# Feature-major product: a block's high-part matmuls first, then its low-part matmuls

## The chip, the cores and the metric

The kernel runs on one core of a Trainium2 chip. The metric is the device time in microseconds from launch to end, median of three runs. Every input and output is fp32.

## What is computed

A two-layer model on 256 tokens of width 2048. Layer 0 mixes an HGRN2 recurrence with latent attention, layer 1 is a retention layer; each is followed by a convolution FFN of width 5632 and by a gated per-layer embedding:

```
h = x
for i in range(2):
    u = rmsnorm(h, norm_mix[i])
    h = h + (even_mixer(u, ...) if i == 0 else odd_mixer(u, ...))
    h = h + conv_ffn(rmsnorm(h, norm_ffn[i]), w_gate[i], w_up[i], conv_w[i], conv_b[i], w_down[i])
    gate = sigmoid(rmsnorm(h, norm_ple[i]) @ ple_w_gate[i])
    h = h + (p[i] @ ple_w_proj[i]) * gate
```

What matters here are the large matrix products in it: the projections of both mixers, three products in each FFN and two in each embedding. Some 520 MB of fp32 weights are read from HBM, each value once.

## The kernel before, in words

Activations are kept with the features on the partitions and the 256 tokens (`T`) along the free dimension, in pieces of 128 features. A product in near-fp32 precision is made of matmuls in the type fp32r: each operand is split into a high part (the value rounded to fp32r) and a low part (the rest), and three of the four partial products are summed: high with high, high with low, low with high. An activation piece `x` holds its high part in columns 0 to 255 and its low part in columns 256 to 511.

`load_w` (L136 to L143) brings a block of weights: SP's queue loads `raw` (four buffers), ACT makes the high part `wh` by a cast (L140, three buffers), and DVE makes the low part `wl` by a subtraction (L142, three buffers). `blocks_of` (L145 to L151) yields these blocks for one group of output features, four pieces of the inner dimension to a block (`KB` = 4).

`gemm_fm` (L153 to L166) computes 256 output features, 128 in each of two PSUM banks. For each of the four pieces `kc` of a block and each bank `j` it issues two matmuls, each with a weight load of its own: the high part of the weights with all 512 columns of `x` (L163, here called *hi*), which gives high times high in the bank's first half and high times low in its second, and right behind it the low part of the weights with the 256 high columns of `x` (L164, *lo*), summed into the first half. A block is so eight pairs, hi and lo in turn. In the product of the per-layer input (`px`) the inner dimension has two pieces, and a block is four pairs.

`gemm_fm` serves the output projections of both mixers, the query, key and gate projections of layer 1, all of the FFN's products and the embedding's. Two other products stand beside it: `gemm_fm1` (L168 to L184), in which one bank takes both halves and all matmuls have 256 columns (L178, L180, L181), and `gemm_tm` (L186 to L202), in which the activations are the loaded operand and all matmuls have 512 columns (L197, L198, L199).

After each block `pump()` lets chains of small steps go on (norm statistics, rotary parts, the recurrence, attention), so that their small matmuls (such as L871, L894 and L895 in layer 1) come in between large ones. After a product, `evac` (L204 to L209) adds the halves of a bank by a copy on ACT (L208) and an add on DVE (L209), or `residual` (L310 to L315) adds both halves to `h`. PSUM has five buffers for large products (`mm`) and three for small ones. The order on ACT and DVE is set when the kernel is built and isn't quite the order of the text: the cast of a block stands ahead of the copies of the product before it where there is room.

Of the kernel before, what the change touches and what calls it, by code (L numbers as in the profile page):

```python
# [15 lines left out]
PSUM = bass.MemoryType.PSUM  # L16

P = 128
T = 256
# [10 lines left out]
CH = 64  # L30
# [16 lines left out]

# columns of the packed vectors
_VEC = (
# [12 lines left out]

# columns of the packed constant matrices
_MAT = (
# [12 lines left out]
def hybrid_kernel(ctx, tc, io):  # L77
    nc = tc.nc
# [31 lines left out]

# [1 line left out]
    active = []  # L112
# [21 lines left out]

# [1 line left out]
    def load_w(src, width):  # L136
# [8 lines left out]
    def blocks_of(blocks, n, width, kb, sub=None):  # L145
        """The loaded parts of one group's weights, kb chunks of K in a block, sub of them to a load."""
        sub = sub or kb
        for k0 in range(0, n, sub):
            k1 = min(n, k0 + sub)
            o = (k0 % kb) * width  # L150
            yield range(k0, k1), load_w(blocks[k0 // kb][:, o:o + (k1 - k0) * width], (k1 - k0) * width)  # L151

    def gemm_fm(blocks, xs):  # L153
        """[features, tokens] of 256 features, a bank for each 128: products with the weights' hi (and lo with
        the activations' hi) in columns 0..T, with the activations' lo in columns T..2T."""
        ps = [psum.tile([P, 2 * T], F32, tag="mm", name="mm", bufs=5) for _ in range(2)]
        n = len(xs)
        for ks, (wh, wl) in blocks_of(blocks, n, 2 * P, KB):
            for kc in ks:
                x = xs[kc]  # L160
                for j in range(2):
                    o = ((kc - ks[0]) * 2 + j) * P
                    nc.tensor.matmul(ps[j], wh[:, o:o + P], x, start=(kc == 0), stop=False)  # L163
                    nc.tensor.matmul(ps[j][:, 0:T], wl[:, o:o + P], x[:, 0:T], start=False, stop=(kc == n - 1))  # L164
            pump()
        return ps  # L166

    def gemm_fm1(blocks, xs, ncol=2, kb=KB, sub=None):  # L168
        """[features, tokens] of ncol * 128 features in one bank."""
        ps = psum.tile([P, ncol, T], F32, tag="mm", name="mm", bufs=5)  # L170
        n = len(xs)
        for ks, (wh, wl) in blocks_of(blocks, n, ncol * P, kb, sub):
            for kc in ks:
                x = xs[kc]
                for j in range(ncol):
                    o = ((kc - ks[0]) * ncol + j) * P
                    w = wh[:, o:o + P]
                    nc.tensor.matmul(ps[:, j], w, x[:, 0:T], start=(kc == 0 and j == 0), stop=False,  # L178
                                     skip_group_check=True)
                    nc.tensor.matmul(ps[:, j], w, x[:, T:2 * T], start=False, stop=False, skip_group_check=True)  # L180
                    nc.tensor.matmul(ps[:, j], wl[:, o:o + P], x[:, 0:T], start=False,  # L181
                                     stop=(kc == n - 1 and j == ncol - 1), skip_group_check=True)
            pump()
        return ps  # L184

    def gemm_tm(blocks, xs, sub=None):  # L186
        """[tokens, 512 features], a bank for each half of the tokens."""
        ps = [psum.tile([P, 512], F32, tag="mm", name="mm", bufs=5) for _ in range(2)]
        n = len(xs)
        for ks, (wh, wl) in blocks_of(blocks, n, 512, 2, sub):  # L190
            for kc in ks:
                x = xs[kc]
                o = (kc - ks[0]) * 512
                for m in range(2):
                    xh = x[:, m * P:(m + 1) * P]
                    xl = x[:, T + m * P:T + (m + 1) * P]
                    nc.tensor.matmul(ps[m], xh, wh[:, o:o + 512], start=(kc == 0), stop=False)  # L197
                    nc.tensor.matmul(ps[m], xh, wl[:, o:o + 512], start=False, stop=False)  # L198
                    nc.tensor.matmul(ps[m], xl, wh[:, o:o + 512], start=False, stop=(kc == n - 1))  # L199
            if ks[-1] % 4 == 3:  # L200
                pump()
        return ps  # L202

    def evac(ps, dst):  # L204
        """dst = the two halves of each bank added."""
        tmp = npool.tile([P, 2, T], F32, tag="evt", name="evt", bufs=2)
        for j in range(2):
            nc.scalar.copy(tmp[:, j], ps[j][:, T:2 * T])  # L208
            nc.vector.tensor_tensor(dst[:, j], ps[j][:, 0:T], tmp[:, j], op=ALU.add)  # L209
# [7 lines left out]
    def split(dst, src, gain=None):  # L217
        """dst = [hi | lo] of src * gain."""
        if gain is None:
            nc.scalar.copy(dst[:, 0:T], src)  # L220
            nc.vector.tensor_tensor(dst[:, T:2 * T], src, dst[:, 0:T].bitcast(F32), op=ALU.subtract)
        else:
            nc.scalar.activation(dst[:, 0:T], src, AF.Copy, scale=gain)
            nc.vector.scalar_tensor_tensor(  # L224
                dst[:, T:2 * T], src, gain, dst[:, 0:T].bitcast(F32), op0=ALU.mult, op1=ALU.subtract)
# [4 lines left out]
    def rstd_from(ps_col, shape, n, factor=1.0):  # L230
        """(sum of squares / n + eps) ** -0.5 * factor of a small PSUM tile."""
        w = shape[1]
# [8 lines left out]
    def diagonals(r, order):  # L241
        """[hi | lo] of the columns of r, each on a diagonal."""
        n = len(order)
# [11 lines left out]
    def bcast_rows(dg, dst):  # L255
        """dst[:, i * 128 + t] = dg[t, 0, i, t] + dg[t, 1, i, t] on every partition."""
        n = dg.shape[2]
        ps = small([P, 512], "sm_bc")
        for half in range(2):
            nc.tensor.matmul(ps[:, 0:n * P], ones_r, dg[:, half].rearrange("p a b -> p (a b)"),  # L260
                             start=(half == 0), stop=(half == 1))
        nc.scalar.copy(dst, ps[:, 0:n * P])

    def token_stats(acc, n, wait=0):
        """1 / rms of each token from squares [features, any, tokens]: as columns and on every partition."""
        r = {}
# [19 lines left out]
    def norm_squares(i, state):  # L286
        """Squares of one finished pair of chunks of the residual stream."""
        acc = state[0]
# [25 lines left out]

# [1 line left out]
    def sin_of(dst, ang, phase, tpool):  # L316
# [29 lines left out]

# [1 line left out]
    def ffn_and_ple(i, st):  # L348
        rs = token_stats(st[0], D, 2)
        xs = st[1]  # L350
        cw, cb = f"cw{i}", f"cb{i}"
        st = new_norm()
        with tc.tile_pool(name=f"ffn{i}", bufs=2, reuse_waits="tile") as fp:
# [69 lines left out]
            def embed_last(pps):  # L423
                """The last group of all, a chunk at a time, on as short a path as can be."""
                n = NC // 2 - 1
# [24 lines left out]

# [1 line left out]
    def lower_bounds(pool):  # L452
        """Softmax over the two rows of logits: [lower bound, 1 - lower bound]."""
        lbt = pool.tile([P, 4, HG_HEADS], F32, name="lbt", bufs=1)
# [15 lines left out]
    def hgrn_pair(pool, hp, f, q, gt, lbc, hvs, mix):  # L470
        """The recurrence of two heads, in chunks of CH tokens."""
        def t2(tag, bufs=1):
# [53 lines left out]
        yield  # L526
        # states after chunks 0 and 2 from rows 0..63, after chunk 1 from rows 64..127, in banks of their own
        pse = small([P, 2, 2, P], "sm_se")
# [49 lines left out]
    def even_mixer(rs, xs):  # L578
        st = new_norm()
        mix_a, mix_b = {}, {}  # L580
        with tc.tile_pool(name="low", bufs=2) as low:
            kpe = low.tile([P, 1, T], F32, name="kpe", bufs=1)
            with tc.tile_pool(name="l0a", bufs=2) as pool:
# [34 lines left out]

                # low-rank projections and their norms
                def low_rank(ps, n, gain, acc, chunks):  # L620
# [34 lines left out]
    def mla(pool, kpe, ckv, cq, rkv, rqa, mix):  # L655
        """Starts the chains of all heads."""
        cos, sin = rope_t["mla"]
# [11 lines left out]
        def pair_rstd(sq, factor):  # L669
            """1 / rms of each (token, head of a pair) from the squares of both heads."""  # L670
            ps = small([P, 512], "sm_hs")
# [6 lines left out]

        # the keys' rotary part, the same for all heads
        key = {}  # L680
# [129 lines left out]

# [1 line left out]
    def odd_mixer(st):  # L812
# [123 lines left out]

# [1 line left out]
    class Arriving:  # L938
        """Chunks of the normed input, loaded and split on their first use."""
        def __init__(self):  # L940
# [27 lines left out]

# [1 line left out]
def _blocks(w, ncols, kb):  # L970
    """[K, N] -> [N / ncols, K / (kb * 128), 128, kb * ncols]: one contiguous piece for each load."""
    K, N = w.shape
# [4 lines left out]
def _cols(v):  # L977
    """[n * 128] -> [128, n]"""
    return np.asarray(v).reshape(-1, P).T
# [103 lines left out]
```

## Time and profile before

| | us |
|---|---|
| median of three runs | 2906.72 |
| lowest and highest run | 2904.05, 2907.08 |
| the profiled execution, first to last instruction (its span) | 2900.2 |
| TensorE matmul busy | 2888.3 |
| TensorE weight load busy | 2525.0 |
| VectorE (DVE) busy | 1957.8 |
| ScalarE (ACT) busy | 1397.4 |
| GpSimd (POOL) busy | 88.6 |

The times of the runs take in what lies around the span, so the profiled execution is known by its span: 2900.2 us, 6.5 us below the median of the runs. Matmuls are pipelined, so their records overlap, and a matmul's price in a stretch is the distance from its start to the next one's. A line such as L163 has a row for the matmul (PE) and one for its weight load (PEld).

### The profile page before, as it was taken

The numbers are of one execution on the slowest core, as the hardware profiler recorded it, in microseconds if no ns is written. First come the engines' busy times: TensorE is split into PE (matmuls) and PEld (weight loads), VectorE is DVE, ScalarE is ACT, GpSimd is POOL, SyncE is SP. The second block draws the span as 40 slices with busy tenths as digits, with TensorE's granted clock in tenths as the row PEclk, the third lists the DMA queues.
The fourth block names the chain that finished last, engine by engine and source line by source line (L and its number), as shares of the span: only waits on it lengthen the run. The fifth ranks groups of instructions, "written<-read, shape, count | busy, mean of one in ns | idle before, by whom it ended". The sixth has DMA issues, their size and how long they took to land.

```text
span 2900.2 us, 42896 instructions
## 1 busy us (share of the span) xinstructions
PE 2888.3 (100%) x16865; PEld 2525.0 (87%) x16865; DVE 1957.8 (68%) x2857; ACT 1397.4 (48%) x1848; POOL 88.6 (3%) x123
## 2 busy tenths in 40 slices
PE   9999999999999999999999999999999999999999
PEld 7999888888888888888888888888888888888888
DVE  8676777676557766786666556666777655777666
ACT  6554554444334444565444344444444433444444
POOL 2111400000000000000000000000000000000000
PEclk9999999999999999999999999999999999999999
DMA  6444355555555555555555555555555555555554
GB/s 220 170 159 160 103 180 180 191 187 189 185 182 191 185 187 189 177 199 177 177 177 180 188 180 179 174 176 188 191 184 182 191 186 188 187 183 190 186 185 167
DMA packets 148812, 525.72 MB, mean 181 GB/s; under 512 B 16640, under 2 KB 18432, under 8 KB 148608
## 3 DMA queue, kind: packets, MB, share of 16 engines
q1 hardware_dynamic: 148608, 522.96, 53.5%
q8 instruction: 132, 2.16, 0.3%
q14 instruction: 72, 0.59, 0.1%
HBM read 520.80 MB, written 2.10 MB: 180 GB/s over the span
## 4 chain that ended last, share of the span: by engine, by line
PE 88%; ACT 0%; DVE 0%; issue 0%
PE mm L163 53%; PE mm L164 27%; PE mm L198 2%; PE mm L197 2%; PE mm L199 2%; PE sm_ro L894 1%; PE sm_ra L871 0%; PE sm_ro L895 0%; PE sm_col L274 0%; PE sm_sc L767 0%; PE sm_bc L260 0%; PE mm L181 0%; PE mm L180 0%; PE mm L178 0%; PE sm_sc L766 0%; PE sm_ao L795 0%
## 5 line engine op out<-in xcount | busy, mean ns | idle before, releaser
L142 DVE TENSOR_TENSOR wl<-raw,wh 128x1024 fp32r<-128x1024 f32 (+1 forms) x1000 | 1206.0, 1210 | 722.9 <-ACT wh L140 721.1
L140 ACT CAST wh<-raw 128x1024 fp32r<-128x1024 f32 (+1 forms) x1000 | 1036.7, 1037 | 1210.7 <-PE mm L163 815.7
L163 PE MATMUL mm<-xs,wh 128*128 128x512 f32 x4320 | 1527.8, 398 | 0.0
L164 PE MATMUL mm<-xs,wl 128*128 128x256 f32 x4320 | 1212.4, 281 | 0.0
L163 PEld LDWEIGHTS mm<-xs,wh 128*128 128x128 f32 x4320 | 811.6, 188 | 199.6
L164 PEld LDWEIGHTS mm<-xs,wl 128*128 128x128 f32 x4320 | 815.7, 189 | 0.3
L163 PE MATMUL mm<-hs,wh 128*128 128x512 f32 x1408 | 497.6, 397 | 0.0
L164 PE MATMUL mm<-hs,wl 128*128 128x256 f32 x1408 | 395.6, 281 | 0.0
L163 PEld LDWEIGHTS mm<-hs,wh 128*128 128x128 f32 x1408 | 264.7, 188 | 65.4
L164 PEld LDWEIGHTS mm<-hs,wl 128*128 128x128 f32 x1408 | 264.3, 188 | 0.0
L208 ACT COPY evt<-mm 128x256 f32<-128x256 f32 x302 | 111.3, 374 | 205.7 <-PE mm L164 205.7
L163 PE MATMUL mm<-xo,wh 128*128 128x512 f32 x512 | 179.9, 393 | 0.0
L178 PE MATMUL mm<-xs,wh 128*128 128x256 f32 x560 | 160.0, 286 | 0.5 <-ACT wh L140 0.5
L181 PE MATMUL mm<-xs,wl 128*128 128x256 f32 x560 | 158.6, 283 | 0.5 <-DVE wl L142 0.4
L180 PE MATMUL mm<-xs,wh 128*128 128x256 f32 x560 | 158.4, 283 | 0.0
L164 PE MATMUL mm<-xo,wl 128*128 128x256 f32 x512 | 144.9, 283 | 0.0
L198 PE MATMUL mm<-wl,xs 128*128 128x512 f32 x320 | 125.7, 393 | 2.7 <-DVE wl L142 2.6
L199 PE MATMUL mm<-wh,xs 128*128 128x512 f32 x320 | 124.8, 391 | 0.6 <-DVE xs L224 0.6
L197 PE MATMUL mm<-wh,xs 128*128 128x512 f32 x320 | 124.5, 391 | 0.0
L163 PEld LDWEIGHTS mm<-xo,wh 128*128 128x128 f32 x512 | 96.2, 188 | 22.1
L178 PEld LDWEIGHTS mm<-xs,wh 128*128 128x128 f32 x560 | 107.3, 192 | 1.6 <-ACT wh L140 0.9
L181 PEld LDWEIGHTS mm<-xs,wl 128*128 128x128 f32 x560 | 107.3, 192 | 0.8 <-DVE wl L142 0.8
(264 smaller groups left out, 2369.9 us busy)
## 6 DMA issues: line engine op xcount, KB each, us to landing
raw<-in_wg SPq DMA_DIRECT2D x176, 512.0 KB, 3.3
raw<-in_wu SPq DMA_DIRECT2D x176, 512.0 KB, 4.1
raw<-in_wd SPq DMA_DIRECT2D x176, 512.0 KB, 4.0
raw<-in_w_oqk SPq DMA_DIRECT2D x64, 512.0 KB, 3.3
raw<-in_w_ov SPq DMA_DIRECT2D x64, 512.0 KB, 3.3
raw<-in_w_og SPq DMA_DIRECT2D x64, 512.0 KB, 3.2
raw<-in_w_oo SPq DMA_DIRECT2D x64, 512.0 KB, 3.2
raw<-in_wpg SPq DMA_DIRECT2D x60, 512.0 KB, 3.9
```

The lines of the kernel that those rows point to most:

```text
L140: nc.scalar.copy(wh, raw)
L142: nc.vector.tensor_tensor(wl, raw, wh.bitcast(F32), op=ALU.subtract)
L163: nc.tensor.matmul(ps[j], wh[:, o:o + P], x, start=(kc == 0), stop=False)
L164: nc.tensor.matmul(ps[j][:, 0:T], wl[:, o:o + P], x[:, 0:T], start=False, stop=(kc == n - 1))
L178: nc.tensor.matmul(ps[:, j], w, x[:, 0:T], start=(kc == 0 and j == 0), stop=False, skip_group_check=True)
L180: nc.tensor.matmul(ps[:, j], w, x[:, T:2 * T], start=False, stop=False, skip_group_check=True)
L181: nc.tensor.matmul(ps[:, j], wl[:, o:o + P], x[:, 0:T], start=False, stop=(kc == n - 1 and j == ncol - 1), skip_group_check=True)
L197: nc.tensor.matmul(ps[m], xh, wh[:, o:o + 512], start=(kc == 0), stop=False)
L198: nc.tensor.matmul(ps[m], xh, wl[:, o:o + 512], start=False, stop=False)
L199: nc.tensor.matmul(ps[m], xl, wh[:, o:o + 512], start=False, stop=(kc == n - 1))
L208: nc.scalar.copy(tmp[:, j], ps[j][:, T:2 * T])
L894: nc.tensor.matmul(pso[:, j], v[:, b, 0, d], at[:, c, 0:T], start=(n == 0), stop=False)
```

## The change

Within a loaded block, the loop over the pieces and banks is run twice: first with all hi matmuls, then with all lo matmuls. The operands, the banks, the columns and the flags of each matmul stay as they were: `start` on the first piece's hi, `stop` on the last piece's lo. The order of the sums in a bank changes with the order of the matmuls. Comments and docstrings were dropped as well, which changes no instruction.

```diff
     def gemm_fm(blocks, xs):
...
         for ks, (wh, wl) in blocks_of(blocks, n, 2 * P, KB):
             for kc in ks:
-                x = xs[kc]
                 for j in range(2):
                     o = ((kc - ks[0]) * 2 + j) * P
-                    nc.tensor.matmul(ps[j], wh[:, o:o + P], x, start=(kc == 0), stop=False)
-                    nc.tensor.matmul(ps[j][:, 0:T], wl[:, o:o + P], x[:, 0:T], start=False, stop=(kc == n - 1))
+                    nc.tensor.matmul(ps[j], wh[:, o:o + P], xs[kc], start=(kc == 0), stop=False)
+            for kc in ks:
+                for j in range(2):
+                    o = ((kc - ks[0]) * 2 + j) * P
+                    nc.tensor.matmul(ps[j][:, 0:T], wl[:, o:o + P], xs[kc][:, 0:T], start=False, stop=(kc == n - 1))
             pump()
         return ps
```

## Rows read from the trace of the kernel before

**Rows 1.** The page: the span, TensorE's busy time, the granted clock by slices.
```profile
span 2900.2 us, 42896 instructions
...
PE 2888.3 (100%) x16865; PEld 2525.0 (87%) x16865; DVE 1957.8 (68%) x2857; ACT 1397.4 (48%) x1848; POOL 88.6 (3%) x123
...
PEclk9999999999999999999999999999999999999999
```

**Rows 2.** The page: the chain that ended last, by engine and line.
```profile
PE 88%; ACT 0%; DVE 0%; issue 0%
PE mm L163 53%; PE mm L164 27%; PE mm L198 2%; PE mm L197 2%; PE mm L199 2%; PE sm_ro L894 1%; PE sm_ra L871 0%; PE sm_ro L895 0%; PE sm_col L274 0%; PE sm_sc L767 0%; PE sm_bc L260 0%; PE mm L181 0%; PE mm L180 0%; PE mm L178 0%; PE sm_sc L766 0%; PE sm_ao L795 0%
```

**Rows 3.** Groups by line: form, count | busy us, mean ns | idle before.
```profile
L163 PE MATMUL mm<-xs,wh 128*128 128x512 f32 x4320 | 1527.8, 398 | 0.0
L164 PE MATMUL mm<-xs,wl 128*128 128x256 f32 x4320 | 1212.4, 281 | 0.0
L164 PEld LDWEIGHTS mm<-xs,wl 128*128 128x128 f32 x4320 | 815.7, 189 | 0.3
```

**Rows 4.** Line L163 alone: its matmuls by moving operand, with counts.
```profile
L163 PE MATMUL mm<-xs,wh x4320: 388/398/476, 442.3 to 2882.4; 128*128 128x512 f32 x197
...
L163 PE MATMUL mm<-hs,wh x1408: 388/397/398, 714.2 to 2792.8; 128*128 128x512 f32 x176
...
L163 PE MATMUL mm<-xo,wh x512: 387/396/398, 1602.0 to 2046.1; 128*128 128x512 f32 x171
...
L163 PE MATMUL mm<-xa,wh x128: 388/398/501, 333.6 to 396.7; 128*128 128x512 f32 x128
...
L163 PE MATMUL mm<-xb,wh x128: 395/398/403, 397.1 to 441.9; 128*128 128x512 f32 x128
...
L163 PE MATMUL mm<-px,wh x64: 389/397/398, 1189.1 to 2883.8; 128*128 128x512 f32 x64
```

**Rows 5.** Timeline of TensorE, `gemm_fm`: start us, length us, instruction (56 pairs).
```profile
2299.95 0.40 PE L163 MATMUL mm<-xs,wh 128*128 128x512 f32 x1
2300.19 0.28 PE L164 MATMUL mm<-xs,wl 128*128 128x256 f32 x1
2300.31 0.40 PE L163 MATMUL mm<-xs,wh 128*128 128x512 f32 x1
...
2319.74 0.40 PE L163 MATMUL mm<-hs,wh 128*128 128x512 f32 x1
```

**Rows 6.** Timeline, `gemm_tm`: the first and, 18 matmuls on, the last.
```profile
126.92 0.39 PE L199 MATMUL mm<-wh,xs 128*128 128x512 f32 x1
...
131.00 0.39 PE L199 MATMUL mm<-wh,xs 128*128 128x512 f32 x1
```

**Rows 7.** Timeline, `gemm_fm1`: the first and, 60 matmuls on, the last.
```profile
159.99 0.28 PE L178 MATMUL mm<-xs,wh 128*128 128x256 f32 x1
...
167.19 0.28 PE L178 MATMUL mm<-xs,wh 128*128 128x256 f32 x1
```

**Rows 8.** Timeline, `gemm_tm` behind small matmuls: second matmul and, eight on, the tenth.
```profile
1396.84 0.39 PE L199 MATMUL mm<-wh,xs 128*128 128x512 f32 x1
...
1398.68 0.39 PE L198 MATMUL mm<-wl,xs 128*128 128x512 f32 x1
```

**Rows 9.** Timeline, `gemm_tm` with `x_kva`: one matmul and, nine on, another.
```profile
303.73 0.39 PE L199 MATMUL mm<-wh,x_kva 128*128 128x512 f32 x1
...
305.82 0.40 PE L199 MATMUL mm<-wh,x_kva 128*128 128x512 f32 x1
```

**Rows 10.** Timeline, L894 and L895 in turn: one pair and, eight pairs on, another.
```profile
1341.22 0.33 PE L894 MATMUL sm_ro<-rat,rv 128*128 128x256 f32 x1
...
1343.07 0.34 PE L894 MATMUL sm_ro<-rat,rv 128*128 128x256 f32 x1
```

**Rows 11.** Waits: who waited for whom, us in total, times, longest us.
```profile
ACT wh L140 <- PE mm L163: 815.7, 487, 2.2
...
ACT evt L208 <- PE mm L164: 205.7, 135, 2.1
...
PE mm L198 <- DVE wl L142: 2.6, 5, 0.9
```

**Rows 12.** Stretch 400 to 440 us: us, busy time by engine, clock, DMA share, GB/s.
```profile
400.00:440.00 40.00, 40.00 (x228) 34.67 (x227) 35.38 (x62) 24.41 (x36) 0.00 (x0) 1.00 0.54 184
```

## The prediction

> **What bounds the kernel now.** Read the page from the top. TensorE is busy for 2888.3 of the 2900.2 us of the span, at a granted clock of full speed (9 in every slice, the 2.4 GHz level) [rows 1]. A busy TensorE is not yet the bound, since matmul records overlap, so the chain of waits comes next: 53% of the span hangs on L163 and 27% on L164, the two matmuls of `gemm_fm`, and no DMA and hardly any ACT or DVE step stands in it [rows 2]. The chain runs from one matmul to the next, so what counts is how far apart matmuls *start*, not how long one is: the mean records of 398 and 281 ns [rows 3] add up to 679 ns, far more than a pair really takes. The counts [rows 4] give 4320 + 1408 + 512 + 128 + 128 + 64 = 6560 pairs of one hi matmul (512 columns) and one lo matmul (256 columns).
>
> The timeline gives the price of a pair. Between the hi matmuls at 2299.95 and 2319.74 us lie 56 pairs in turn: 19.79 / 56 = 353.4 ns each; the first of them shows 0.24 us from hi to lo and 0.12 from lo to the next hi [rows 5]. The chain agrees: 80% of 2900.2 us over 6560 pairs is 354 ns. I use **353 ns**. So the change touches 6560 x 0.353 = 2316 us, and each ns in a pair is worth 6.56 us.
>
> **The change, part by part.**
>
> *Matmuls, weight loads, transfers, casts.* None is added or taken away: 6560 hi and 6560 lo matmuls, each with its own weight load, before and after. SP's queue and POOL's get nothing new. The only direct price is in the start-to-start distances, since hi now follows hi and lo follows lo, in runs of eight (four in the small product with `px`).
>
> *Hi after hi.* `gemm_tm` does just this: 512 columns after 512 columns, a new weight load for each. Settled, 18 of its distances take 131.00 - 126.92 = 4.08 us, 226.7 ns each [rows 6]. Just after matmuls of another size it is slower: the eight distances from 1396.84 to 1398.68 us take 1.84 us, 230 ns each, before it settles [rows 8]. In one stage it does not settle in the stretch shown: nine distances in 305.82 - 303.73 = 2.09 us, 232 ns each [rows 9]. Bounds: 226.7 and 232. I take **230**, since here each run is eight long and starts behind eight of another size, which is the case of rows 8.
>
> *Lo after lo.* `gemm_fm1` has 256 columns after 256 columns, again each with its own load: 60 distances in 167.19 - 159.99 = 7.20 us, **120 ns** each [rows 7]. That a weight load can be hidden behind so short a matmul is seen there: the load's record is 189 ns [rows 3], but loads overlap, and one goes through every 120 ns. How close that is to the load's own limit, L894 and L895 show: a 256-column and a 128-column matmul in turn take 1343.07 - 1341.22 = 1.85 us for eight pairs, 231 ns for two loads, 116 ns for one [rows 10], though 128 columns are streamed much faster than 256. So I read 116 as about the least distance of two loads; 120 lies 4 ns above. Bounds for lo: 116 and 128 (for the upper end, 120 plus the 8 ns by which a hi in turn exceeds a settled one, 235 against 227; 235 is the 353 less the 118 between 0.12 and 0.116).
> The Trainium skill bears on this in "TensorE: Matmul & The Clock Gate", section "LDWEIGHTS (loading the stationary operand)": a load costs its column count over 1.2 GHz, 107 ns for 128 columns; the 116 ns of rows 10 are 9 above it, and by 107 a run of lo matmuls would have more margin, with the same sum.
>
> *The sum.* A pair costs 230 + 120 = 350 ns in place of 353: 3 x 6.56 = **20 us less**. Fully settled it would be 346.7 ns, 6.3 x 6.56 = 41 us less; with the slow hi runs of rows 9 it would be 352 ns, 7 us less; with lo at 116 and hi settled 343 ns, 66 us less, which I hold for unlikely, as the 256-column rows that exist stand at 120.
>
> *The waits on the weights.* The first lo of a block used to come 0.24 us after its first hi and now comes after eight, 8 x 0.23 = 1.8 us. So `wl` may arrive 1.6 us later, and `wh` is free about 8 x 0.12 = 1.0 us sooner, for the cast three loads on. Neither is worth anything now: TensorE's largest wait on DVE's `wl` is 2.6 us, and that at L198, none at L163 or L164, while the casts wait 815.7 us for TensorE and not the other way about [rows 11]. What is queued behind the cast on ACT (the copies of L208) moves a little forward. I cost this at nothing, and the cover is wide: in the densest stage DVE is busy 35.38 of 40.00 us, while TensorE still has no gap [rows 12]; blocks that come 1% faster take DVE from 88 to 89% there.
>
> *The end of a product.* The last matmul into the first bank now comes 0.12 us ahead of the product's end and came 0.353 ahead. So the first copy of `evac` or the first add of `residual` starts 0.23 us later. ACT waits for this end 135 times, 205.7 us in all, without TensorE waiting for it in turn [rows 11]. It could reach TensorE only where a small product waits for the product just done, once a head in layer 1: 8 x 0.23, under 2 us. I leave it in the range.
>
> The profiled execution has a span of 2900.2 us, and the median of the runs is 2906.72; the 6.5 us between lie outside the first and last instruction and are not touched. So the forecast is 2906.7 - 20 = **2887 us**.
>
> **The rivals.**
>
> *Order is worth nothing, 2907 us.* The 8 ns too many of a hi in turn may belong to the products and not to the order: with `x_kva` a run of 512 columns takes 232 ns [rows 9], and 232 + 121 is 353 again. Then the time stays. Against it: rows 6 and rows 7 are two long stretches at 227 and 120, in other stages, and the pairs in turn lie above their sum. Another road to the same result is that the reordering doesn't reach the engine in long runs, since small products get in between; but within a block they are few. Chance 0.17.
> [...]
>
> *Fully settled, 2866 us.* Runs settle at once: 226.7 + 120 = 346.7, 41 us less. For it: rows 6 and 7 are the states that last. Against it: rows 8 shows that eight matmuls pass before the state is reached. Chance 0.25, on the same side as the forecast.
>
> *Slower: the weight loads become the bound in the runs of lo.* In turn, two loads share 353 ns; in a run of lo matmuls each has 120. A load that comes in behind a lo must be in place before the next can stream. If it needs 128 ns there (the 8 ns that a hi behind a lo is late now, read as a load not yet done), every lo waits: 230 + 128 = 358 ns, 5 x 6.56 = 33 us more, **2940 us**. The point from which it decides is a lo run above 123 + 1 = 124 ns. For it: the hi matmul that is late now is the one whose load has only a lo to hide behind. Against it: 256 columns after 256 run at 120 in rows 7 with the same kind of loads, and rows 10 put two loads at 116. If nothing of the load overlapped, at 189 ns [rows 3], the time would be over 3300 us, which rows 7 exclude. Chance 0.09.
>
> **How the numbers follow.** The forecast, 350 ns a pair and up to 2 ns beside it, has 0.49. A measurement of this kernel can tell about 0.2% from no change, 5.8 us, so faster means below 2900.9 us, or more than 0.9 ns off a pair. The forecast and the settled case are both faster, 0.74; the no-change rival is 0.17, and slower is 0.09. The range runs from the settled case with 3 us below it (2863) to the no-change rival with its scatter (2908); outside it lie the slower rival and the part of the settled case in which lo runs reach 116, less than 2 in 10 together.
>
> **What would show it.** Right: in the timeline of the changed kernel eight L163-type starts about 0.23 us apart, then eight L164-type starts 0.12 apart, 2.80 us for a block in place of 2.83; the share of the two lines in the chain a little under 80%; no wait of TensorE on `wh` or `wl`. The no-change rival would show hi runs at 0.232 or more, the settled case 0.227. The slower rival would show lo starts 0.125 us or more apart. The casts' wait for TensorE should name the end of the hi run, and begin earlier in the block. It would all be wrong if TensorE showed gaps at block ends, where I expect none, or if the granted clock left full speed.

## The result and the profile after

The changed kernel runs in **2881.09 us** (median of four, 2879.67 to 2883.60), the kernel before beside it in 2905.39 (2903.19 to 2907.08): a ratio of **0.9925, 95% interval 0.9913 to 0.9937**, which is 18 to 25 us less. The spans of the two profiled executions differ by 2900.2 - 2879.1 = 21.1 us. The forecast was 20 us less.

In the changed kernel the hi matmuls are at L162, the lo matmuls at L166. The page's first lines and its chain, against [rows 1, 2]:

```profile
span 2879.1 us, 42907 instructions
...
PE 2867.2 (100%) x16865; PEld 2522.5 (88%) x16865; DVE 1945.5 (68%) x2857; ACT 1399.7 (49%) x1848; POOL 95.6 (3%) x123
...
PEclk9999999999999999999999999999999999999999
...
PE mm L162 53%; PE mm L166 27%; PE mm L201 2%; PE mm L200 2%; PE mm L199 2%; PE sm_ro L896 1%; PE sm_ra L873 0%; PE sm_ro L897 0%; PE sm_col L276 0%; PE sm_sc L769 0%; PE sm_bc L262 0%; PE mm L183 0%; PE mm L180 0%; PE mm L182 0%; PE sm_sc L768 0%; PE sm_ao L797 0%
```

TensorE has as many matmuls and loads as before, and it lost 21 us of busy time, as much as the span. So the matmuls themselves come closer together.

One place differs in a way that the page hides, since one of its slices is 72 us long. Three hi into a block TensorE waits ahead of a small matmul, 1.52 us for DVE where it waited 0.72 for ACT before (first row, of the kernel before). Then, from 343.46 us on, the granted clock is 0.50 of full speed (the last row: a stretch as in [rows 12]), the 1.2 GHz level, for 3.41 us; before, it stayed at full speed there:

```profile
340.53 0.49 PE L766 MATMUL sm_sc<-kn,qn 128*128 128x128 f32 x2 [0.72 <-ACT rk L262]
...
340.28 0.49 PE L768 MATMUL sm_sc<-kn,qn 128*128 128x128 f32 x2 [1.52 <-DVE xb L223]
...
343.28 2.33 PE L162 MATMUL mm<-xa,wh 128*128 128x512 f32 x5
345.41 1.77 PE L166 MATMUL mm<-xa,wl 128*128 128x256 f32 x8
...
343.46:346.87 3.41, 3.41 (x12) 2.92 (x12) 2.58 (x14) 1.18 (x2) 1.56 (x2) 0.50 0.00 0
```

The five hi take 2.13 us there, 426 ns each. The longer wait and the lower clock cost about 0.8 + 1.7 = 2.5 us.

How much closer the matmuls come, the timeline of TensorE shows, where runs now stand as one row each (start us, length, line, count). With `xs` as the moving operand, against [rows 5]:

```profile
2061.11 2.00 PE L162 MATMUL mm<-xs,wh 128*128 128x512 f32 x8
2062.95 1.11 PE L166 MATMUL mm<-xs,wl 128*128 128x256 f32 x8
2063.90 2.00 PE L162 MATMUL mm<-xs,wh 128*128 128x512 f32 x8
```

From the first hi to the first lo are 1.84 us, 230 ns for each of eight, and on to the next hi 0.95 us, 119 ns for each: 2.79 us a block, 349 ns a pair. With `hs`:

```profile
1102.12 2.02 PE L162 MATMUL mm<-hs,wh 128*128 128x512 f32 x8
1103.98 1.07 PE L166 MATMUL mm<-hs,wl 128*128 128x256 f32 x8
1104.89 1.32 PE L162 MATMUL mm<-hs,wh 128*128 128x512 f32 x5
```

Here hi takes 232 ns and lo 114, 2.77 us a block, 346 ns a pair. And with `xo`:

```profile
1613.22 2.03 PE L162 MATMUL mm<-xo,wh 128*128 128x512 f32 x8
1615.09 1.12 PE L166 MATMUL mm<-xo,wl 128*128 128x256 f32 x8
1616.04 2.02 PE L162 MATMUL mm<-xo,wh 128*128 128x512 f32 x8
```

That is 2.82 us, 352 ns a pair. So the products gain differently. Over all starts in the two traces (hi distances under 280 ns and lo distances under 180, so that interruptions by other work are left out), a pair went from 352.8 to 349.1 with `xs`, from 353.3 to 346.7 with `hs`, and from 351.2 to 351.3 with `xo`. That makes 4320 x 3.7 + 1408 x 6.6 = 25 us, a little more than was measured; some 5 us go back to interruptions, below. Why `hs` gains most and `xo` nothing was not foreseen, and half of the experiments are about it.

The waits after (who waited for whom, us in total, times, longest), against [rows 11]:

```profile
ACT wh L140 <- PE mm L162: 957.7, 620, 3.3
...
DVE h L314 <- PE mm L166: 72.9, 62, 1.6
```

The casts wait for the end of the hi run, as forecast, 957.7 us where they waited 815.7. The wait of ACT's copies for the last matmul of a product, 205.7 us before, is gone altogether: ACT now spends its spare time at the casts. DVE's first adds of `residual` (L314) wait 72.9 us for the last lo, 17.3 before; no wait of TensorE names them.

### The profile page after: what moved, and what is told of

Same layout as the page of the kernel before. It is cut to its first block, busy times and chain, and to the rows that moved or that the text cites. A ratio compares the mean times of both kernels' runs of the same rounds, so it can differ in the third digit from the quotient of the medians.

```text
span 2879.1 us, 42907 instructions
## 1 busy us (share of the span) xinstructions
PE 2867.2 (100%) x16865; PEld 2522.5 (88%) x16865; DVE 1945.5 (68%) x2857; ACT 1399.7 (49%) x1848; POOL 95.6 (3%) x123
## 4 chain that ended last, share of the span: by engine, by line
PE 88%; DVE 0%; ACT 0%; issue 0%
PE mm L162 53%; PE mm L166 27%; PE mm L201 2%; PE mm L200 2%; PE mm L199 2%; PE sm_ro L896 1%; PE sm_ra L873 0%; PE sm_ro L897 0%; PE sm_col L276 0%; PE sm_sc L769 0%; PE sm_bc L262 0%; PE mm L183 0%; PE mm L180 0%; PE mm L182 0%; PE sm_sc L768 0%; PE sm_ao L797 0%
## 5 line engine op out<-in xcount | busy, mean ns | idle before, releaser
L140 ACT CAST wh<-raw 128x1024 fp32r<-128x1024 f32 (+1 forms) x1000 | 1035.4, 1036 | 1360.8 <-PE mm L162 957.7
L162 PE MATMUL mm<-xs,wh 128*128 128x512 f32 x4320 | 1086.2, 393 | 0.0
L162 PEld LDWEIGHTS mm<-xs,wh 128*128 128x128 f32 x4320 | 775.7, 189 | 142.8 <-DVE sg L211 4.7
L166 PEld LDWEIGHTS mm<-xs,wl 128*128 128x128 f32 x4320 | 589.2, 190 | 42.3
L166 PE MATMUL mm<-xs,wl 128*128 128x256 f32 x4320 | 602.2, 282 | 0.0
L162 PE MATMUL mm<-hs,wh 128*128 128x512 f32 x1408 | 356.2, 395 | 0.0
L162 PEld LDWEIGHTS mm<-hs,wh 128*128 128x128 f32 x1408 | 251.5, 188 | 47.0
L166 PEld LDWEIGHTS mm<-hs,wl 128*128 128x128 f32 x1408 | 186.9, 188 | 16.0
L166 PE MATMUL mm<-hs,wl 128*128 128x256 f32 x1408 | 189.1, 277 | 0.0
L183 PE MATMUL mm<-xs,wl 128*128 128x256 f32 x560 | 158.6, 283 | 0.2 <-DVE wl L142 0.2
L162 PE MATMUL mm<-xo,wh 128*128 128x512 f32 x512 | 129.7, 395 | 0.0
L180 PEld LDWEIGHTS mm<-xs,wh 128*128 128x128 f32 x560 | 107.3, 192 | 0.7
L183 PEld LDWEIGHTS mm<-xs,wl 128*128 128x128 f32 x560 | 107.3, 192 | 0.5 <-DVE wl L142 0.4
L182 PEld LDWEIGHTS mm<-xs,wh 128*128 128x128 f32 x560 | 107.4, 192 | 0.2
L162 PEld LDWEIGHTS mm<-xo,wh 128*128 128x128 f32 x512 | 91.8, 188 | 16.9
L314 DVE TENSOR_TENSOR h<-h,mm 128x256 f32<-128x256 f32 x128 | 48.2, 418 | 72.9 <-PE mm L166 72.9
```

The lines of the kernel that those rows point to most:

```text
L140: nc.scalar.copy(wh, raw)
L162: nc.tensor.matmul(ps[j], wh[:, o:o + P], xs[kc], start=(kc == 0), stop=False)
L166: nc.tensor.matmul(ps[j][:, 0:T], wl[:, o:o + P], xs[kc][:, 0:T], start=False, stop=(kc == n - 1))
L314: nc.vector.tensor_tensor(h[i][:, j], h[i][:, j], ps[j][:, 0:T], op=ALU.add)
```

## The experiments

A pair's time below is the mean over a whole trace, taken as above; the rows shown are one stretch of it. All ratios are to the kernel before on the same chip.

### Is it the bank, the late load, or the change of width?

Three causes for the extra 7 to 8 ns of a hi in turn are tried: that a lo adds into the bank that the hi just wrote (the bank theory), that the load for a hi is late behind a short lo (the late load), and the change of width itself, after which a run of one width must settle.

`lag1` keeps hi and lo in turn, but shifts lo by one pair, so that a lo no longer follows a hi into the same bank. (The hi right behind that lo now does go into the lo's bank, so the words "never share a bank" below do not hold for the whole block.)

```diff
+            pairs = [(kc, j) for kc in ks for j in range(2)]
+
+            def lo(p):
+                kc, j = pairs[p]
+                nc.tensor.matmul(ps[j][:, 0:T], wl[:, p * P:(p + 1) * P], xs[kc][:, 0:T], start=False, stop=(kc == n - 1))
+            for p, (kc, j) in enumerate(pairs):
+                nc.tensor.matmul(ps[j], wh[:, p * P:(p + 1) * P], xs[kc], start=(kc == 0), stop=False)
+                if p:
+                    lo(p - 1)
+            lo(len(pairs) - 1)
```

> Hi and lo still in turn, but each lo follows the hi of the next pair, so that neighbours never share a bank; the changes of width are as many as before but for two in a block. If what counts is that a lo adds into the bank that the hi just wrote (bank theory): as fast as the changed kernel, 2881 us. If the change of width, or a weight load late behind a short lo, is the cost: about as slow as the kernel before, 2900 to 2905 us, with hi near 235 ns.

Measured: 2900.33 us, ratio 0.9992 (0.9982 to 1.0001); 352.5 ns a pair with `hs`, 352.1 with `xs`. The bank theory, that a lo pays for adding into the bank that the hi just wrote, falls: without that, hi and lo in turn are as slow as before. That neighbours in one bank cost nothing in general is shown only by `run2_other_x`, below.

`turn384` leaves the order of the kernel before and widens lo to 384 columns, which adds the low-times-low product for half of the tokens:

```diff
-                    nc.tensor.matmul(ps[j][:, 0:T], wl[:, o:o + P], x[:, 0:T], ...)
+                    nc.tensor.matmul(ps[j][:, 0:T + P], wl[:, o:o + P], xs[kc][:, 0:T + P], ...)
```

> Hi and lo in turn as before, but lo takes 384 columns (it adds the low-times-low product for half of the tokens), so that the load for the next hi has 160 ns of streaming to hide behind in place of 107. Late load: hi falls from 235 to 227 ns, lo takes 173, a pair 400 ns, 47 more than before, about 3214 us. Change of width as such, or the bank: hi stays at 235, a pair is 407 ns, about 3260 us.

Measured: 3268.66 us (one run). The timeline, from one hi to the hi 49 pairs on:

```profile
2599.97 0.39 PE L162 MATMUL mm<-hs,wh 128*128 128x512 f32 x1
2600.19 0.34 PE L163 MATMUL mm<-hs,wl 128*128 128x384 f32 x1
...
2619.89 0.39 PE L162 MATMUL mm<-hs,wh 128*128 128x512 f32 x1
```

19.92 / 49 = 406.5 ns a pair, where 400 were due if only the load had been late. 128 more columns take 53.3 ns (by [rows 6] and [rows 7], 226.7 - 120 ns for 256 columns), and on the 353.3 that `hs` takes in turn they give 406.6. So the extra in turn stays in the sum when the load has half as much again to hide behind: the late load falls too. Its sign for hi alone did come in part: over the trace a hi with `hs` fell from 235.0 to 230.3 ns, but lo rose to 176.4, 4.7 more than the added columns explain.

`turn512` makes lo as wide as hi, in turn (the whole low-times-low product is added):

```diff
-                    nc.tensor.matmul(ps[j][:, 0:T], wl[:, o:o + P], x[:, 0:T], ...)
+                    nc.tensor.matmul(ps[j], wl[:, o:o + P], xs[kc], ...)
```

> Hi and lo in turn, with all 512 columns in both (the low-times-low product is added), so that the width never changes while the weights still come from wh and wl in turn and two loads of different tiles alternate. If the change of width in turn is the cost: 226.7 ns each, 453.3 a pair, 100 more than before, about 3560 us. If alternating the two weight tiles is the cost: the 6.7 ns stay, 460 ns a pair, about 3605 us.

Measured: 3592.04 us (one run), between the two. The timeline with `xs`, 22 pairs, and with `hs`, 21 pairs:

```profile
999.63 0.39 PE L162 MATMUL mm<-xs,wh 128*128 128x512 f32 x1
...
1009.60 0.39 PE L162 MATMUL mm<-xs,wh 128*128 128x512 f32 x1
```

```profile
899.77 0.39 PE L162 MATMUL mm<-hs,wh 128*128 128x512 f32 x1
...
909.57 0.39 PE L162 MATMUL mm<-hs,wh 128*128 128x512 f32 x1
```

9.97 / 22 = 453.2 ns with `xs`, the settled pace of [rows 6] twice over, and 9.80 / 21 = 466.7 with `hs`. Loading from `wh` and `wl` in turn costs nothing by itself, then, since with `xs` nothing is left over. But the operand that is fastest in runs is the slow one here: with `hs` 512 columns take 233.3 ns, as hi did in the changed kernel (232.7 over the trace), where only lo was fast (114.0). Something that belongs to the operand takes part, and it acts on 512 and on 256 columns differently.

### How long must a run be?

`run2` issues both banks' hi of a piece, then both banks' lo:

```diff
             for kc in ks:
                 for j in range(2):
...
                     nc.tensor.matmul(ps[j], wh[:, o:o + P], xs[kc], start=(kc == 0), stop=False)
-            for kc in ks:
                 for j in range(2):
...
                     nc.tensor.matmul(ps[j][:, 0:T], wl[:, o:o + P], xs[kc][:, 0:T], start=False, stop=(kc == n - 1))
```

> Runs of two: both banks' hi, then both banks' lo. Late load (each hi right behind a lo pays 8 ns, no other): half of the hi pay, 350 ns a pair, about 2886 us. Settling (a run of hi needs some six matmuls to reach 227 ns, the first two take 234 and 236): 235 + 117 = 352 ns, about 2897 us. Bank theory: 2881 us.

Measured: **2874.21 us**, ratio 0.9897 (0.9882 to 0.9912), below all three expectations and below runs of eight. With `hs`, eight groups of two pairs:

```profile
1099.85 0.62 PE L162 MATMUL mm<-hs,wh 128*128 128x512 f32 x2
1100.31 0.39 PE L165 MATMUL mm<-hs,wl 128*128 128x256 f32 x2
...
1105.40 0.62 PE L162 MATMUL mm<-hs,wh 128*128 128x512 f32 x2
```

5.55 / 16 = 347 ns a pair (346.7 over the trace); `xs` has 348.5, `xo` 348.6. Runs of two have four times the changes of width of runs of eight and are not slower here. So a change of width shows no price of its own, and the picture of a run that must settle first does not explain the gain. What is expensive is strict turn, with a neighbour of another width on either side of each matmul: `xo`, which gained nothing in runs of eight, takes 351.2 in turn and 348.6 in runs of two.

`run16` takes lo first in every second block, so that runs join across blocks:

```diff
+            for part in ("hl" if ks[0] // KB % 2 == 0 else "lh"):
+                for kc in ks:
+                    for j in range(2):
...
```

> Every second block takes its lo matmuls first, so that runs are sixteen long with the same buffers. Late load: one hi in sixteen pays, 0.5 ns a pair less than runs of eight, 2878 us. Settling: the second eight of a run stand at 226.7 and 120, 348 ns a pair with xs in place of 349.2, about 2873 us. Bank theory: 2881 us. If the lo parts come too late for a block that begins with them, TensorE shows gaps and it is slower than 2881.

Measured: 2872.09 us, ratio 0.9893 (0.9876 to 0.9909), what settling gave. The timeline with `xs`, three double blocks of sixteen pairs each:

```profile
2061.12 3.82 PE L164 MATMUL mm<-xs,wh 128*128 128x512 f32 x16
2064.78 2.08 PE L167 MATMUL mm<-xs,wl 128*128 128x256 f32 x16
2066.69 3.82 PE L164 MATMUL mm<-xs,wh 128*128 128x512 f32 x16
...
2077.82 2.46 PE L164 MATMUL mm<-xs,wh 128*128 128x512 f32 x10
```

16.70 / 48 = 347.9 ns, where 348 was expected. But `hs` stays at 346.7 and `xo` at 351.4, as in runs of eight. So settling is real with `xs` and absent with the two others.

`run2_other_x` forms its runs of two from two pieces into one bank, so that neighbours don't share the moving operand:

```diff
+            for k in range(0, len(ks), 2):
+                for j in range(2):
+                    for kc in ks[k:k + 2]:
...
```

> Runs of two as in the kernel with both banks' hi and then both banks' lo (346.7 ns a pair with hs, 348.5 with xs, 2874 us), but the two of a run now take two different pieces of the activations into the same bank, so that no two neighbours in a run read the same moving columns. If a width that comes at least twice in a row is enough: the same, 2872 to 2877 us. If it is the repeated moving operand that makes the runs cheap: the gain goes, 352 to 353 ns a pair, about 2900 us, and in the changed kernel, where each piece is read twice in a row, it would be the same cause.

Measured: 2875.51 us, ratio 0.9908 (0.9893 to 0.9923); 346.7 and 348.4 ns with `hs` and `xs`. Reading the same columns twice is not the cause. And neighbours in one bank cost nothing: three of four neighbours share a bank here, a hi and the lo behind it among them, and none did in `run2`.

### Why the operands differ: where they lie

By the addresses that the build gives the tiles, a weight piece in `wh` or `wl` starts 64 bytes past a multiple of 256 in its partition, `hs` at a multiple of 256, `xs` 64 past one and `xo` 192 past one. Call moving operand minus weights, modulo 256, the *distance*: -64 for `hs`, 0 for `xs`, 128 for `xo`. Two kernels with small unused tiles in front of the pools (set to zero once, in lines not shown) tell whether that is what matters. `run8_x0` moves the operands:

```diff
+    pad_x = cpool.tile([P, 48], F32, name="pad_x")
...
+    pad_w = wpool.tile([P, 16], F32, tag="pad_w", name="pad_w", bufs=1)
...
+            pad_l = l1.tile([P, 16], F32, tag="pad_l", name="pad_l", bufs=1)
```

> The changed kernel with pads of 64 to 192 bytes, so that every moving operand of gemm_fm starts at a multiple of 256 bytes in its partition, as hs alone did (xs, xa and xb stood 64 bytes past one, xo 192), and wh and wl stay 64 past one. If the start address sets which runs settle: xs goes from 349.1 to 346.7 ns and xo from 351.3 to 346.7, 4320 x 2.4 + 512 x 4.6 = 13 us less than the changed kernel, about 2868 us. If hs was faster for another reason (its stage, its neighbours): 2881 us, xs still at 349.1.

Measured: 2868.31 us, ratio 0.9881 (0.9866 to 0.9896), and 347.1 ns with `xs`, 346.8 with `xo`, 346.7 with `hs`. That is 13 us less than the changed kernel, for three unused tiles.

`run8_w128` moves the weights instead:

```diff
+    pad_w = wpool.tile([P, 16], F32, tag="pad_w", name="pad_w", bufs=1)
...
+    pad_n = npool.tile([P, 48], F32, tag="pad_n", name="pad_n", bufs=1)
```

> The changed kernel with wh and wl moved by 64 bytes, to 128 past a multiple of 256, and all moving operands where they were (hs 0, xs 64, xo 192). If the distance between the moving operand and the weights counts: xs now stands 64 below the weights, as hs did, and falls to 346.7, while hs (128 below) rises to about 351; about 4320 x 2.4 - 1408 x 4.3 = 4 us less, 2877 us. If the moving operand's own address counts: hs stays at 346.7, xs at 349.1, xo at 351.3, 2881 us.

Measured: 2872.22 us, ratio 0.9898 (0.9882 to 0.9915). The timeline with `hs`, two blocks, and with `xo`, two blocks:

```profile
1102.19 2.02 PE L166 MATMUL mm<-hs,wh 128*128 128x512 f32 x8
1104.05 1.10 PE L170 MATMUL mm<-hs,wl 128*128 128x256 f32 x8
...
1107.81 2.02 PE L166 MATMUL mm<-hs,wh 128*128 128x512 f32 x8
```

```profile
1613.88 1.99 PE L166 MATMUL mm<-xo,wh 128*128 128x512 f32 x8
1615.71 1.11 PE L170 MATMUL mm<-xo,wl 128*128 128x256 f32 x8
...
1619.39 1.99 PE L166 MATMUL mm<-xo,wh 128*128 128x512 f32 x8
```

`hs`, not moved at all, goes from 346.7 to 5.62 / 16 = 351 ns, since its distance is now -128, which modulo 256 is the 128 that `xo` had; `xs` (now -64) falls to 347.1. Each operand takes the pace that its distance had with another operand before, so the distance counts, not the address and not the product. `xo` shows a distance not seen so far, 64: 5.51 / 16 = 344 ns (345.1 over the trace), the fastest.

So the last four put every operand of `gemm_fm` at one distance, again by pads alone: 64 with runs of eight, in turn, and with runs of two, and 32 with runs of eight. The pads for 64 (for 32 they are 8, 56, 24 and 40 columns; the order in `gemm_fm` is that of the kernel named):

```diff
+    pad_x = cpool.tile([P, 16], F32, name="pad_x")
...
+    pad_w = wpool.tile([P, 48], F32, tag="pad_w", name="pad_w", bufs=1)
...
+            pad_f = fp.tile([P, 32], F32, tag="pad_f", name="pad_f", bufs=1)
...
+            pad_l = l1.tile([P, 48], F32, tag="pad_l", name="pad_l", bufs=1)
```

> The changed kernel with every moving operand of gemm_fm placed 64 bytes above the weights (modulo 256), the distance at which xo ran at 345.1 ns a pair when the weights were moved. If the distance alone sets the pace of a run: 345.1 ns for all operands, 6560 x 4.3 = 28 us less than the changed kernel at 349.4, about 2855 us. If xo's 345.1 belonged to that product: 346.7 to 349, 2866 to 2881 us.

> The kernel before (hi and lo in turn) with the same distance of 64 bytes above the weights. In turn, distances of -64, 0 and 128 gave 353.3, 352.8 and 351.2 ns. If the order is what counts and the distance a second-order matter in turn: 351 to 353 ns, 2892 to 2905 us. If the distance counts as much as the order: 345 to 347 ns, 2855 to 2868 us, and then the gain of the change would hang on where the tiles happen to lie.

> Runs of two at the same distance. Runs of two stood at 346.7 (distance -64), 348.5 (0) and 348.6 (128), runs of eight at 346.7, 349.1 and 351.3: runs of two never worse. If that holds here: 345 ns or a little less, 2850 to 2856 us. Otherwise the short run pays for its changes of width: 347 to 349 ns, 2868 to 2878 us.

> The changed kernel with the moving operands 32 bytes above the weights. If the pace changes in steps of 64 bytes, it goes with one neighbour: with distance 0, 349.1 ns (2880 us), or with 64, 345.1 (2855 us). If it changes evenly with the distance: 347 ns, 2867 us.

Measured: `run8_p64` **2855.29 us**, ratio 0.9837 (0.9823 to 0.9852); `turn_p64` 2904.88 us, ratio 1.0007 (0.9997 to 1.0016); `run2_p64` 2856.06 us, ratio 0.9840 (0.9825 to 0.9854); `run8_p32` 2894.73 us, ratio 0.9973 (0.9961 to 0.9984). The timelines with `xs`: two blocks in runs of eight at 64,

```profile
2041.06 1.99 PE L166 MATMUL mm<-xs,wh 128*128 128x512 f32 x8
2042.88 1.11 PE L170 MATMUL mm<-xs,wl 128*128 128x256 f32 x8
...
2046.57 1.99 PE L166 MATMUL mm<-xs,wh 128*128 128x512 f32 x8
```

54 pairs in turn at 64,

```profile
2060.84 0.39 PE L166 MATMUL mm<-xs,wh 128*128 128x512 f32 x1
...
2079.92 0.39 PE L166 MATMUL mm<-xs,wh 128*128 128x512 f32 x1
```

and three blocks in runs of eight at 32:

```profile
2060.31 2.03 PE L166 MATMUL mm<-xs,wh 128*128 128x512 f32 x8
2062.18 1.10 PE L170 MATMUL mm<-xs,wl 128*128 128x256 f32 x8
...
2068.73 2.03 PE L166 MATMUL mm<-xs,wh 128*128 128x512 f32 x8
```

5.51 / 16 = 344 ns, 19.08 / 54 = 353 ns, and 8.42 / 24 = 351 ns. At 64 the order alone is worth 353.2 - 344.8 = 8.4 ns a pair. At 32 the pace is that of neither neighbour, and of none of the three expectations: slower than both 0 and 64, so it doesn't change evenly.

All together, ns a pair, mean over the trace, with the operand and the kernel it is from:

| distance, bytes | in turn | runs of 2 | runs of 8 | runs of 16 |
|---|---|---|---|---|
| -64 (`hs`) | 353.3, before | 346.7, run2 | 346.7, changed | 346.7, run16 |
| 0 (`xs`) | 352.8, before | 348.5, run2 | 349.1, changed | 348.1, run16 |
| 32 (`xs`) | not tried | not tried | 350.8, run8_p32 | not tried |
| 64 (`xs`) | 353.2, turn_p64 | 345.3, run2_p64 | 344.8, run8_p64 | not tried |
| 128 (`xo`) | 351.2, before | 348.6, run2 | 351.3, changed | 351.4, run16 |

The first column is flat: in turn a pair takes 351 to 353 ns wherever the operands lie. The others are not: runs allow a faster pace, and how much of it is reached hangs on the distance. `run8_p64` and `run2_p64` beat both kernels, and there runs of two are 0.5 ns a pair behind runs of eight.

The pads move the operands of the other products too, and these change their pace although nothing in their order was touched. In `gemm_tm`, where the weights move and the activations are loaded, 512 columns with `xs` take 227.0 ns at a distance of 0 (before), 229.2 at 64 (run8_w128) and 233.4 at -64 (turn_p64), the mean from the ninth matmul of a run on. A stretch of `turn_p64`, against [rows 6]:

```profile
127.07 0.40 PE L201 MATMUL mm<-wl,xs 128*128 128x512 f32 x1
...
131.27 0.40 PE L201 MATMUL mm<-wl,xs 128*128 128x512 f32 x1
```

18 distances take 4.20 us, 233.3 ns each, which is the pace of `hs`, also at -64, in `turn512`. In `gemm_fm1`, 256 columns with `xs` take 120.1 ns at 0 (before) and 116.0 at 64 (run8_p64). In `run8_p64`, where `gemm_tm` stands at -64, the two nearly cancel: 960 x 6.4 = 6 us lost, 1680 x 4.1 = 7 us won.

## Why the prediction was right

**The bound.** Right. TensorE's starts were the bound and stayed it; little but their distances changed, and the chain's two shares are the same. A gap of TensorE at block ends or a clock below full speed was named as the sign that all was wrong. A longer wait inside a block and a lower clock did come, between 338 and 347 us, but they cost 2.5 of 2879 us: the sign was too strict.

**The size.** 350 ns a pair was forecast, and 348.8 came as the mean over all products: with `xs` hi at 230.1 (230 forecast) and lo at 119.0 (120). The stretch of [rows 8] was the right one for `xs`: eight hi take 1.84 us in both. But the nearest row fitted because `gemm_tm` in [rows 8] has the same distance, 0, between its operands as `gemm_fm` has with `xs`, and that was not seen. With `hs` the terms are 232.7 and 114.0, and it is the sum that helps; with `xo` nothing is gained. An average of three different paces met the forecast, so the closeness of the number is in part luck.

**What a run of eight stands for.** The step "each run is eight long and starts behind eight of another size, which is the case of rows 8" took the run's length as the reason. Runs of two are better or within 0.5 ns, so this failed as a reason. [Rows 9], where `x_kva` ran at 232 and did not settle, was read as a matter of the stage; by the build's addresses its distance is 128, at which `xo` gains nothing. `run8_w128` moves it to -64, and it stays slow, at 233.5, as `xs` is in the same product at -64; no kernel here brought it to 0 or 64.

**The load's own limit.** The 116 ns that were read from [rows 10] as about the least distance of two loads were too high: lo runs with `hs` go at 114.0 ns on average over 1408. The slower rival, which needed 124, was so further off than thought, and `turn384` speaks, by the sum, against its mechanism.

**The waits on the weights.** Right: no wait of TensorE for a cast or a subtraction at L162 or L166.

**The end of a product.** Wrong, and small. The first copy of `evac` was to start 0.23 us later. By the semaphores that the build sets, it still waits for the last lo, but ACT loses nothing there any more: the cast in front of the copies waits for the end of the hi run and takes 1.05 us, and by then the lo run, 0.95 us long, is over. The end of one product and the start of the next:

```profile
2659.77 1.11 PE L166 MATMUL mm<-xs,wl 128*128 128x256 f32 x8
2659.97 1.05 ACT L140 CAST wh<-raw 128x1024 fp32r<-128x1024 f32 x1 [1.70 <-PE mm L162]
...
2660.72 2.04 PE L162 MATMUL mm<-hs,wh 128*128 128x512 f32 x8
2660.92 0.64 ACT L210 COPY evt<-mm 128x256 f32<-128x256 f32 x2
```

What is new is a wait of hi's loads for the adds of `evac`:

```profile
PEld mm L162 <- DVE sg L211: 4.7, 13, 0.4
```

These 13 are in the embedding, where a product of few pieces comes between large ones: with hi right behind hi the second bank is wanted 0.12 us sooner after the first, and it is not yet read out. In all, TensorE's distances of 280 ns and more after a hi came to 63 where they had been 30, and to 7.8 us above the usual 231 ns where they had been 2.3: 2.6 us of it in the embedding, 2.7 us at the wait and the lower clock of 338 to 347 us, and 2.5 us around the small matmuls, about as before. So some 5 of the 25 us that the undisturbed pairs gain went back; the sum had up to 2 us for the end of a product, and nothing for the wait and the clock.

**The rivals.** "Order is worth nothing" is true of one operand, `xo`, and there of runs of eight alone. The Trainium skill ("TensorE: Matmul & The Clock Gate", section "Back-to-back issue gap") gives the gap of an isolated matmul as its columns over 2.4 GHz and 2.5 ns more; an estimate by it for 512 and 256 columns is 325 ns in any order. The page itself sets this apart from a stream in which every matmul has its load, as here, and the runs took 344.8 to 353.3 ns by order and place. "Fully settled" at 346.7 is the pace that `hs` has, but by other terms (232.7 + 114.0 in place of 226.7 + 120), and it is no floor: 344.8 was reached.

What stays open is the mechanism: no run here shows why the distance counts, why it slows 512 columns and speeds 256 at -64, or why strict turn hides it.

## What to carry to other kernels

Where matmuls are bound by their starts, group those of one width, at least two at a time: strict turn of 512 and 256 columns cost 4 to 8 ns in 350 at three of the four distances that were tried both ways, and groups of two gain about as much as groups of eight. Then look at where the operands lie: other pads, of 32 to 224 bytes, moved the grouped kernel from 2881 to 2855 or to 2895 us, at the best as much as the change itself. Such pads act on every product that shares the tiles, and one of them can lose what another wins, as `gemm_tm` did. A row of the trace taken as the price of a new pattern should match it in operand placement too, not only in shape.

## What the runs showed of the hardware that was not expected

- The start-to-start distance of fp32r matmuls with a weight load each depends on the distance between the moving operand's and the weights' start addresses, modulo 256 bytes: 344.8 ns a pair at 64, 346.7 at -64, 349.1 at 0, 350.8 at 32 and 351.3 at 128, all in runs of eight. 512 columns alone take 227 ns at 0, 229 at 64 and 233 at -64 in `gemm_tm`.
- In strict turn the extra over the grouped order is 6.6 ns with `hs`, and it seems not to shrink where lo is longer: lo with 256 columns takes 353.3 a pair and with 384 columns 406.7, the 53.3 of 128 columns more (the grouped order with 384 columns was not run).
- A weight load of 128 columns, with a record of 188 ns, goes through every 114 ns behind 256-column matmuls.
- In 8 of the 14 traces the granted clock fell to 0.50 of full speed, the 1.2 GHz level, at 337 to 345 us, for 3.4 to 10.2 us, after TensorE had waited 0.8 to 1.6 us for a small step; in the other six it did not, after waits of 0.7 to 1.5 us at the same place. What decides is not shown. At 10.2 us (0.50 from 338.46 to 348.69 us in `run8_p64`) it costs about 5 us by estimate, so a few us between two kernels can come from it alone.
